# Turning the rotated keys and queries with transposing DMAs on planes of 16-bit words

## The chip, the cores and the metric

The kernel runs on one core of one Trainium2 chip. The metric is the device time of one execution in microseconds, taken as the median of repeated runs. A run's profile gives a span, from the first to the last instruction, which is a little shorter than the device time. The engines are called as in the profile: PE is TensorE's matmul side and PEld its weight loads, DVE is VectorE, ACT is ScalarE, POOL is GpSimd, and SP is SyncE, which only issues DMAs here.

## The reference

The reference is a two-layer decoder trunk on 256 tokens of width 1024, all in float32. Layer 0 is a gated short convolution, a cross-attention to 256 memory tokens and a SwiGLU. Then the residual stream gives one shared set of keys and values (8 heads of 128). Layer 1 is a block-sparse causal attention that reads them, a second cross-attention and a second SwiGLU. At 256 tokens the block-sparse attention has a single block, so it is plain causal attention inside that block. What matters here, cut to its core:

```python
k, v = jnp.split(rms_norm(x, kv_norm) @ w_kv, 2, axis=-1)
k = apply_partial_rope(k.reshape(bsz, seq, N_HEADS, HEAD_DIM), cos, sin)
q = apply_partial_rope((h @ w_q).reshape(bsz, seq, N_HEADS, HEAD_DIM), cos, sin)
...
s_own = jnp.einsum("bhqd,bhkd->bhqk", q_c, k_own).astype(jnp.float32) * scale
```

The rotation touches the first 32 of each head's 128 features. The products of queries and keys contract over the 128 features, so both operands are needed with features on the partitions, while the projections leave tokens on the partitions. The step between the two is a transposition of 128x128 float32 blocks, and that step is what the change rewrites.

## The kernel before

Every large product is done with three matmuls on split operands: each operand is a high part (rounded to the matmul's float32r) and a low part (the rest), and a product is high x low, low x high and high x high (`mm3`, line 338). Weights come in chunks of 128 rows x 1024 columns (512 KB): a load on SP's queue into one of 5 raw buffers, a high part written by ACT, a low part written by DVE (`split_high`, `split_low`), and both parts go into one of 10 weight buffers (`WBUFS`).

The program is written as one long order of PE work. Beside it a planner in Python keeps an estimated clock for each engine (`Clock`), and puts all other work in between. Side jobs are generators (`Side`): a job emits some instructions, yields, and is taken up again when the planner's clock says that they are done. After nearly every matmul the planner polls the jobs that are due, and then lets the weight feed go on (`Feed.pump`): one low part if DVE is free by the planner's clock, and one high part if ACT is. A pause can stand in the feed's way:

```python
    # Side.poll, lines 146-147
        soon = any(self.clock.now <= i[0] <= self.clock.now + HOLD for i in self.open)
        self.feed.pump(soon)
    # Feed.pump, lines 214-215
        if soon and sum(it["halves"] for it in self.items[self.taken:self.lows]) >= AMPLE:
            return
    # arrived, lines 316-318
        while clock.ready(ap) > clock.now != seen:
            seen = clock.now
            yield 200
```

`HOLD` is 300 ns and `AMPLE` is 2. A job that has yielded a number of nanoseconds is due that much later, so `soon` says that some job is due within 300 ns. `halves` is 1 for each chunk of the projections k1, q1 and v1. `taken` counts the chunks that PE has begun to use and `lows` those that are split completely. If a chunk is wanted that has not been split, `Feed.take` emits its missing parts at once. When a low part is emitted, the load of the chunk five further on follows on SP's queue (`load_to`), where it waits until DVE has read the raw buffer.

The stage around the change is `moba` (line 1480). It runs the projections k1, q1 and v1 one after the other with `proj_rows`: token half h=0 over all 8 chunks, each chunk for both column banks b=0 and 1, and then h=1 over the same chunks, of which the first five bankwise together and the last three bank by bank. So a projection takes its 8 chunks in its first half, 6 matmuls each, and takes none in its second half, in which the chunks are given back one after the other. Each of the four results (h, b) of k1 and q1 is 128 tokens x 512 features, which is four heads. `turn` evicts it with ACT into the tile `r`, with the normalisation's factor, rotates it in place on DVE (four instructions, tile `rope`), turns its four 128x128 blocks with four PE transposes into one PSUM bank (`pt_r`), and copies that bank into `kT` or `qT`: on ACT for b=0, on DVE for b=1. There are 8 such turns. `attend` (line 1517) is started for (h, pair of heads) from the beginning of v1 on, 4000 ns apart by the planner's clock; it needs the turned keys and queries of its heads and, later, the values. The "half" tiles, 8 of them, hold `r` and the softmax's tiles.

DMA is booked by the planner as well: a weight load takes 1.55 ns for each of its 1024 columns (line 350), one after the other, and the DRAM-to-DRAM copies that prepare sums of weights for a later stage (lines 464 and 466, tile `T`) take 1460 or 3300 ns.

Of the kernel before, what the change touches and what calls it, by code (L numbers as in the profile page):

```python
# [12 lines left out]
F32R = mybir.dt.float32r  # L13
BF16 = mybir.dt.bfloat16
I32 = mybir.dt.int32
AF = mybir.ActivationFunctionType
OP = mybir.AluOpType
AX = mybir.AxisListType

P = 128  # L20
# [65 lines left out]
class Timed:  # L86
# [5 lines left out]
    def __getattr__(self, op):  # L92
        call = getattr(self.engine, op)

        def issue(out, *args, **kw):
# [5 lines left out]
            for func in args:  # L101
                if func in (AF.Exp, AF.Silu, AF.Sin) and func != self.clock.table:
                    self.clock.table = func
# [160 lines left out]
def yoco_kernel(  # L264
# [6 lines left out]
    nc = tc.nc  # L271
# [16 lines left out]
    clock = Clock()  # L288
    vector, scalar, pool = (Timed(clock, n, e) for n, e in
                            (("dve", nc.vector), ("act", nc.scalar), ("pool", nc.gpsimd)))  # L290
    side = Side(clock, tp=2, gu=2, half=HALVES, pair=PAIRS)
# [8 lines left out]
    def tp_tile(name):  # L300
        return ps_tp.tile([P, 4, P], F32, tag="tp", name=name)
# [5 lines left out]
    def held_half(name, shape=(P, 512)):  # L307
        return halves.tile(list(shape), F32, tag="half", name=name)
# [4 lines left out]
    def arrived(ap):  # L313

        seen = None
# [3 lines that stand above are left out]
# [4 lines left out]
    def tok(h):  # L323
        return slice(h * P, (h + 1) * P)
# [9 lines left out]
    def transpose(o, i):  # L334
        nc.tensor.transpose(o, i, ident[:i.shape[0], :i.shape[0]])
        clock.note("pe", 109, [o], [i], 200)
# [55 lines left out]
    def split_high(it, raw):  # L392
        hi = wts.tile([P, it["a"], it["b"]], F32R, tag="hi", name=f"hi_{it['name']}")
        lo = wts.tile([P, it["a"], it["b"]], F32R, tag="lo", name=f"lo_{it['name']}")
        for c in chunk_pieces(it):
            if it["gain"] is None:
                scalar.copy(hi[:, :, c], raw[:, :, c])
            else:
                scalar.activation(hi[:, :, c], raw[:, :, c], AF.Copy, scale=gain_col(*it["gain"]))
        return hi, lo  # L400
# [150 lines left out]
    def proj_rows(act, name, done, order=STRAIGHT):  # L551

        chunks, accs = {}, {}
        for h, k, b in order:
            if (h, b) not in accs:
                accs[h, b] = acc_tile(f"acc_{name}_{h}_{b}")
            if k not in chunks:
                chunks[k] = feed.take(f"{name}_{k}")
            if h == 1 and b == 1:
                feed.free()  # L560
            mm_rows(accs[h, b], act, k, h, chunks[k], b, k == 0, k == KD - 1)
            if k == KD - 1:
                done(h, b, accs[h, b])

    def turn_parts(src, dst, h, g, gain=None):

# [25 lines left out]
    def square_half(src, ss, b):  # L592
        junk = small.tile([P, 512], BF16, tag="junk", name="junk", bufs=2)
        scalar.activation(junk[:, :src.shape[1]], src, AF.Square, accum_out=ss[:, b:b + 1])

# [12 lines left out]
    def keep(dst, acc, scale, b):  # L608
        if b == 0:
            scalar.activation(dst, acc, AF.Copy, scale=scale)  # L610
        else:
# [15 lines left out]
    def gain_col(name, k):  # L627
        i = GAINS.index(name) * KD + k
        return g_cols[:, i:i + 1]
# [26 lines left out]
    class Turned:  # L656
# [24 lines left out]
        def turn(self, i, t):  # L681
            yield from arrived(t)
            for k in range(2):
                scalar.activation(t[:, k, :], t[:, k, :], AF.Copy, scale=gain_col(self.gain, 2 * i + k))
            yield
# [140 lines left out]
    def mem_values(name, mT):  # L826
        vs = [acts.tile([P, 2, D], F32R, tag="unit", name=f"{name}_{h}") for h in range(2)]

        def keep_parts(h, b, acc):
            hi, lo = (vs[h][:, r, bank(b)] for r in range(2))  # L830
            scalar.activation(hi, acc, AF.Copy, scale=m_rs[:, h:h + 1])
            yield
# [84 lines left out]
    def angles():  # L917
        freq = const.tile([P, HR], F32, name="freq")
        for i in range(HR):
            nc.gpsimd.memset(freq[:, i:i + 1], inv_freq[i])  # L920
        pos_i = const.tile([P, 2], I32, name="pos_i")
        with nc.allow_non_contiguous_dma(reason="256 positions"):
# [557 lines left out]
    def moba(src, into):  # L1480
        act = src.act
        kT = unit_f32("kT", [P, NH, T])
        v_sb = unit_f32("v_sb", [P, 2, D])
        qT = unit_f32("qT1", [P, NH, T])
        scale = P ** -0.5
        turning, attending = {}, {}

        def turned(dst, key):

            def turn(h, b, acc, r):  # L1490
                scalar.activation(r, acc, AF.Copy, scale=rstd[h])
                yield
                v = r.rearrange("p (n d) -> p n d", d=P)
                t = small.tile([P, 2, 4, ROT], F32, tag="rope", name="rope", bufs=1)
                for i in range(2):
                    vector.tensor_mul(t[:, i], v[:, :, :ROT], cs[:, h, i:i + 1, :].to_broadcast([P, 4, ROT]))
                vector.tensor_sub(v[:, :, :HR], t[:, 0, :, :HR], t[:, 1, :, HR:])
                vector.tensor_add(v[:, :, HR:ROT], t[:, 0, :, HR:], t[:, 1, :, :HR])
                yield
                yield from side.hold("tp")  # L1500
                pt = tp_tile("pt_r")
                for i in range(4):
                    transpose(pt[:, i, :], r[:, i * P:(i + 1) * P])
                side.give("half")
                yield
                d = dst[:, 4 * b:4 * b + 4, tok(h)]
                if b:
                    vector.tensor_copy(d, pt)
                else:
                    scalar.copy(d, pt)  # L1510
                side.give("tp")

            def done(h, b, acc):
                turning[key, h, b] = side.start(turn(h, b, acc, half_tile("r")))
            return done

        def attend(h, hp, oT):
            m = (h + 1) * P
            for hh in range(h + 1):
                for key in "qk":  # L1520
                    side.finish(turning[key, hh, hp // 2])
            yield from side.hold("gu")
            s = gu_tile("s1")
            for i in range(2):
                n = 2 * hp + i
                mm(s[:, i, :m], qT[:, n, tok(h)], kT[:, n, :m], True, True, 218 * (h + 1))
            yield
            own = s[:, :, h * P:m]
            vector.tensor_add(own, own, causal[:, None, :].to_broadcast([P, 2, P]))
            yield from side.hold("half")  # L1530
            p = held_half("p1", (P, 2, T))
            yield from softmax(s[:, :, :m], p[:, :, :m], scale, -scale)
            yield from side.hold("tp")
            pt = tp_tile("pt1")
            for i in range(2):
                for kt in range(h + 1):
                    transpose(pt[:, 2 * i + kt, :], p[:, i, kt * P:(kt + 1) * P])
            side.give("half")
            yield from side.hold("half")
            pT = held_half("pT1", (P, 2, 2, P))  # L1540
            yield
            scalar.copy(pT[:, :, :h + 1, :], pt.rearrange("p (i k) t -> p i k t", i=2)[:, :, :h + 1, :])
            side.give("tp")
            yield
            c = slice(hp * 2 * P, (hp + 1) * 2 * P)
            while any((hh, hp // 2) not in v_jobs or clock.ready(v_sb[:, hh, c]) > clock.now for hh in range(h + 1)):
                yield 100
            yield from side.hold("tp")
            po = tp_tile("po1")
            for i in range(2):  # L1550
                n = 2 * hp + i
                for kt in range(h + 1):
                    mm(po[:, i, :], v_sb[:, kt, n * P:(n + 1) * P], pT[:, i, kt, :], kt == 0, kt == h, 218)
            side.give("half")
            yield
            u, j0 = oT.units[hp // 2], 2 * (hp % 2)
            yield from split_steps(u[:, j0:j0 + 2, 0, tok(h)], u[:, j0:j0 + 2, 1, tok(h)], po[:, :2, :])

        proj_rows(act, "k1", turned(kT, "k"))
        proj_rows(act, "q1", turned(qT, "q"))  # L1560
        mT1 = Act(side, [])

        def mem_bank(g):
            mT1.units.append(acts.tile([P, 4, 2, T], F32R, tag="unit", name=f"mT1_{g}"))
            nc.gpsimd.dma_start(mT1.units[g], mem_aside[g])

        mem_bank(0)
        oT = new_act("oT_moba")

        def attend_all():  # L1570
            yield 1500
            for h in range(2):
                for hp in range(4):
                    attending[h, hp] = side.start(attend(h, hp, oT))
                    yield 4000

        every = side.start(attend_all())
        v_jobs = {}

        def keep_v(h, b, acc):  # L1580
            keep(v_sb[:, h, bank(b)], acc, rstd[h], b)
            v_jobs[h, b] = True

        proj_rows(act, "v1", keep_v)
        mem_bank(1)
        memk1 = mem_keys("memk1", mT1, (1, 1, 3000, 6000))
        side.finish(every)
        for job in attending.values():
            side.finish(job)
        proj_rows(oT, "o1", residual(into))  # L1590
        return memk1, mT1
# [81 lines left out]
```

## Time and profile before

| what | value |
|---|---|
| device time, median of 3 runs | 788.64 us (787.6 to 789.31) |
| profiled execution, span | 785.8 us, 11249 instructions |
| profiled execution, own total time | not listed by the profile; the timed runs lie 1.8 to 3.5 us above the span |
| busy: PE, PEld | 775.1 us (99%), 664.4 us (85%) |
| busy: DVE, ACT, POOL | 572.7 us (73%), 458.3 us (58%), 41.5 us (5%) |
| DMA | 182.71 MB, mean 233 GB/s |
| first matmul of k1, q1, v1, memk1 | 387.5, 411.1, 435.1, 465.3 us |

Busy shares are means over the whole span. A row of a timeline reads: start in us, duration in us, engine, line of the kernel, operation, output <- inputs, shape, and how many instructions were merged; a bracket gives the idle time before it and what ended it. A row of a group reads: busy time in us and mean ns of one. The lines 107, 331, 335 and 348 are those of helpers that record every DVE, ACT or POOL instruction, every matmul, every PE transpose and every load, so a reader goes by the tiles' names. The chain of waits is followed back from the last instruction, and gives for each piece what the end of the program hung on at that time.

### The profile page before, as it was taken

What the parts mean: (1) busy time and instruction counts of PE and PEld (TensorE: products, weight loads), DVE (VectorE), ACT (ScalarE), POOL (GpSimd) and SP (SyncE); (2) the same over time, 40 slices, a digit from 0 to 9 for tenths busy, and PEclk for the clock granted to TensorE, in tenths of its full rate; (3) what the DMA queues carried; (4) which work ended last, traced back from release to release, by engine and by line L of the source; (5) the groups of instructions that cost most, each with busy time, mean ns of one, the idle gap of its engine ahead of it and who ended that gap; (6) DMA issues with size and microseconds to landing.
All of it is one profiled execution on the core that took longest, in us unless ns stands there. A gap on an engine that the chain in (4) does not pass through costs nothing.

```text
span 785.8 us, 11249 instructions
## 1 busy us (share of the span) xinstructions
PE 775.1 (99%) x4151; PEld 664.4 (85%) x4151; DVE 572.7 (73%) x863; ACT 458.3 (58%) x728; POOL 41.5 (5%) x68
## 2 busy tenths in 40 slices
PE   8999999999999999999999999999999999999996
PEld 7988888898788888888888889888987888888885
DVE  5988787768687566687766666876767786876874
ACT  6875656575564455566655563655755556655651
POOL 1000001100100000000110010021101000000000
PEclk9999999999999999999999999999999999999999
DMA  8887788926676855699789666989956856856931
GB/s 316 298 272 217 249 303 228 353 75 214 191 235 231 242 170 191 205 346 351 235 246 294 194 160 187 322 229 267 255 185 185 247 175 212 309 193 210 335 119 53
DMA packets 99959, 182.71 MB, mean 233 GB/s; under 512 B 6656, under 2 KB 62976, under 8 KB 99456
## 3 DMA queue, kind: packets, MB, share of 16 engines
q1 hardware_dynamic: 92656, 167.02, 62.4%
q0 software_dynamic: 6816, 14.68, 10.6%
q8 instruction: 32, 0.52, 0.3%
q10 hardware_dynamic: 432, 0.29, 0.1%
q14 instruction: 23, 0.19, 0.1%
HBM read 178.82 MB, written 28.31 MB: 264 GB/s over the span
## 4 chain that ended last, share of the span: by engine, by line
PE 91%; DVE 2%; DMA 1%; issue 1%; ACT 1%; POOLq 0%; DVEq 0%; ACTq 0%
PE gu L331 20%; PE ff L331 14%; PE seven L331 7%; PE q_acc L331 6%; PE acc_mo L331 6%; PE acc_memv L331 6%; PE cu L331 5%; PE acc_memk L331 3%; PE acc_v L331 3%; PE pb L331 3%; PE acc_q L331 3%; PE acc_o L331 3%; PE acc_cout L331 3%; PE acc_k L331 3%; PE po L331 2%; PE s L331 2%
## 5 line engine op out<-in xcount | busy, mean ns | idle before, releaser
L331 PE MATMUL ff<-hi_wd,guT 128*128 128x512 f32 (+1 forms) x352 | 108.3, 388 | 0.0
L331 PEld LDWEIGHTS ff<-hi_wd,guT 128*128 128x128 f32 x352 | 65.8, 188 | 12.8
L331 PE MATMUL ff<-lo_wd,guT 128*128 128x512 f32 (+1 forms) x176 | 68.3, 388 | 0.0
L107 DVE TENSOR_TENSOR gu_sb<-gu_sb,gu 128x256 f32<-128x256 f32 x48 | 20.2, 421 | 56.1 <-ACT gu_sb L107 55.4
L107 ACT COPY gu_sb<-gu 128x256 f32<-128x256 f32 x48 | 17.9, 373 | 72.2 <-PE gu L331 72.1
L107 DVE TENSOR_TENSOR lo_wd<-raw_wd,hi_wd 128x1024 fp32r<-128x1024 f32 x44 | 53.5, 1220 | 2.5 <-ACT hi_wd L107 2.4
L107 ACT CAST hi_wd<-raw_wd 128x1024 fp32r<-128x1024 f32 x44 | 46.0, 1049 | 8.0 <-DMA raw_wd<-in_ffn_w_down_dram 6.7
L331 PE MATMUL gu<-ffn,hi_wg 128*128 128x512 f32 x192 | 48.0, 390 | 0.0
L331 PE MATMUL gu<-ffn,hi_wu 128*128 128x512 f32 x192 | 47.7, 391 | 0.0
L331 PE MATMUL acc_memk<-mT,hi_memk 128*128 128x256 f32 x256 | 46.2, 286 | 0.2 <-ACT hi_memk L107 0.2
L331 PEld LDWEIGHTS gu<-ffn,hi_wg 128*128 128x128 f32 x192 | 35.9, 188 | 7.3
L331 PEld LDWEIGHTS gu<-ffn,hi_wu 128*128 128x128 f32 x192 | 35.7, 188 | 7.2
L331 PE MATMUL gu<-hi_wr,ffn 128*128 128x512 f32 x128 | 40.8, 395 | 0.0
L331 PE MATMUL acc_mo<-hi_mo,oT_mem 128*128 128x512 f32 x128 | 40.6, 393 | 0.0
L107 DVE TENSOR_TENSOR lo_wu<-raw_wu,hi_wu 128x1024 fp32r<-128x1024 f32 x32 | 38.7, 1221 | 2.6 <-ACT hi_wu L107 2.5
L331 PEld LDWEIGHTS acc_memk<-mT,hi_memk 128*128 128x128 f32 x256 | 39.5, 193 | 0.8 <-ACT hi_memk L107 0.6
L331 PE MATMUL acc_memv<-hi_memv,mT 128*128 128x512 f32 x128 | 39.6, 390 | 0.0
L464 POOL DMA_DIRECT2D T<-in_ffn_w_gu_dram x24 | 25.6, 1068 | 256.6 <-DMA T<-in_ffn_w_gu_dram 87.9
L331 PEld LDWEIGHTS ff<-lo_wd,guT 128*128 128x128 f32 x176 | 33.2, 188 | 6.3
L107 ACT CAST hi_wu<-raw_wu 128x1024 fp32r<-128x1024 f32 x32 | 33.6, 1052 | 5.4 <-DMA raw_wu<-in_ffn_w_gu_dram 4.5
L331 PE MATMUL acc_memk<-mT,lo_memk 128*128 128x256 f32 x128 | 35.1, 288 | 0.8 <-DVE lo_memk L107 0.7
L107 POOL TENSOR_TENSOR rs<-ms,neg_half 128x1 f32<-128x1 f32 x14 | 12.3, 878 | 414.7 <-DVE ms L107 414.7
(267 smaller groups left out, 1967.9 us busy)
## 6 DMA issues: line engine op xcount, KB each, us to landing
raw_wd<-in_ffn_w_down_dram SPq DMA_DIRECT2D x44, 512.0 KB, 5.1
T<-in_ffn_w_gu_dram POOLq DMA_DIRECT2D x24, 512.0 KB, 8.4
raw_wg<-in_ffn_w_gu_dram SPq DMA_DIRECT2D x24, 512.0 KB, 5.3
raw_wu<-in_ffn_w_gu_dram SPq DMA_DIRECT2D x24, 512.0 KB, 4.9
raw_wT<-T SPq DMA_DIRECT2D x24, 512.0 KB, 4.9
raw_wB<-in_ffn_w_gu_dram SPq DMA_DIRECT2D x18, 512.0 KB, 5.2
raw_memv<-in_mem_w_kv_dram SPq DMA_DIRECT2D x16, 512.0 KB, 6.2
raw_mq<-in_mem_w_q_dram SPq DMA_DIRECT2D x16, 512.0 KB, 6.3
```

The costliest lines, as they stand in the source:

```text
L107: return call(out, *args, **kw)
L331: nc.tensor.matmul(o, l, r, start=start, stop=stop)
L464: nc.gpsimd.dma_start(dst, src, accum_op=OP.add)
```

## The change

The four PE transposes and the copy out of PSUM go. In their place `turn_by_dma` does this for each of the 8 turns:

1. A DVE copy takes the rotated tile, 128 tokens x 512 float32, as 1024 16-bit words a row, and writes the words into two planes: first all first halves of the numbers, then all second halves (tile `planes`).
2. One transposing DMA, issued from SP's queue, turns the 8 blocks of 128 words of the planes, so that features come to the partitions (tile `turned`).
3. A second DVE copy interleaves the two planes again into `kT` or `qT`.

Both copies are on DVE in all 8 turns. Between the steps the job waits with `arrived`, and the planner books the DMA at 1500 ns and its result at 4000 ns behind that. `attend` no longer finishes the turns that it needs; it waits for them, and for their results, by polling every 200 ns.

```diff
+    def copy_words(engine, out, src, out_f32, src_f32):
+        fixed, each = clock.COST[engine]
+        if engine == "act":
+            nc.scalar.copy(out, src)
+        else:
+            nc.vector.tensor_copy(out, src)
+        clock.note(engine, fixed + each * math.prod(out.shape[1:]), [out_f32], [src_f32])
+
+    def turn_by_dma(src, dst, engines):
+        yield from side.hold("half")
+        flat = held_half("planes")
+        copy_words(engines[0], flat.bitcast(U16).rearrange("p (two n) -> p two n", two=2),
+                   src.bitcast(U16).rearrange("p (n two) -> p two n", two=2), flat, src)
+        side.give("half")
+        yield from side.hold("half")
+        back = held_half("turned")
+        yield from arrived(flat)
+        words = back.bitcast(U16).rearrange("p (b t) -> p b t", t=P)
+        nc.sync.dma_start_transpose(words, flat.bitcast(U16))
+        clock.note("dma", 1500, [back], [flat], 4000)
+        side.give("half")
+        yield from arrived(back)
+        copy_words(engines[1], dst.bitcast(U16).rearrange("p n (t two) -> p two n t", two=2),
+                   words.rearrange("p (two n) t -> p two n t", two=2), dst, back)
+        side.give("half")
+        yield
...
-                yield from side.hold("tp")
-                pt = tp_tile("pt_r")
-                for i in range(4):
-                    transpose(pt[:, i, :], r[:, i * P:(i + 1) * P])
-                side.give("half")
-                yield
-                d = dst[:, 4 * b:4 * b + 4, tok(h)]
-                if b:
-                    vector.tensor_copy(d, pt)
-                else:
-                    scalar.copy(d, pt)
-                side.give("tp")
+                yield from turn_by_dma(r, dst[:, 4 * b:4 * b + 4, tok(h)], ("dve", "dve"))
...
             for hh in range(h + 1):
-                for key in "qk":
-                    side.finish(turning[key, hh, hp // 2])
+                for dst, key in ((qT, "q"), (kT, "k")):
+                    while not turning[key, hh, hp // 2][2]:
+                        yield 200
+                    while clock.ready(dst[:, 2 * hp:2 * hp + 2, tok(hh)]) > clock.now:
+                        yield 200
```

More of the change, by code (lines that the diff above doesn't have):

```diff
@@ L15 @@
 I32 = mybir.dt.int32
+U16 = mybir.dt.uint16
 AF = mybir.ActivationFunctionType
```

## The prediction

> **What bounds the kernel now.** I read the page first, then the chain of waits around the change, then the timelines of ACT and DVE there.
>
> ```profile
> span 785.8 us, 11249 instructions
> PE 775.1 (99%) x4151; PEld 664.4 (85%) x4151; DVE 572.7 (73%) x863; ACT 458.3 (58%) x728; POOL 41.5 (5%) x68
> PE 91%; DVE 2%; DMA 1%; issue 1%; ACT 1%; POOLq 0%; DVEq 0%; ACTq 0%
> ```
>
> PE is busy for 99% of the span and carries 91% of the chain. So PE work that is removed shortens the run, and a PE wait that is added lengthens it; other work counts only when it makes PE wait. The chain in order of time (start, us, what) prices the removed work:
>
> ```profile
> 400.73 0.44 PE pt_r L335 x4
> ...
> 401.64 0.53 PE pt_r L335 x4
> 402.17 9.12 PE acc_k L331 x40
> ...
> 412.43 0.44 PE pt_r L335 x4
> ...
> 413.33 0.44 PE pt_r L335 x4
> 413.77 10.71 PE acc_q L331 x47
> 424.48 0.44 PE pt_r L335 x4
> ...
> 425.38 0.48 PE pt_r L335 x4
> 425.86 9.09 PE acc_q L331 x40
> 434.95 0.44 PE pt_r L335 x4
> ...
> 437.02 0.44 PE pt_r L335 x4
> ```
>
> All eight groups are on the chain: 6 x 0.44 + 0.53 + 0.48 = 3.65 us. Between them PE runs without a gap at 9.12 / 40 = 0.228 us a matmul, so a chunk of weights lasts 6 x 0.228 = 1.37 us in the first half of a projection, and the half lasts 10.9 us. That it has no gap is owed to weights split well ahead:
>
> ```profile
> 391.98 2.19 ACT L107 ACTIVATE hi_q<-raw_q,g_cols 128x1024 fp32r<-128x1024 f32 x2
> 398.79 1.31 ACT L107 ACTIVATE r<-acc_k,rs 128x512 f32<-128x512 f32 x2 [4.62 <-PE acc_k L331]
> 401.21 0.59 ACT L107 COPY kT<-pt_r 128x512 f32<-128x512 f32 x1 [1.11 <-PE pt_r L335]
> 401.69 1.16 ACT L107 ACTIVATE hi_q<-raw_q,g_cols 128x1024 fp32r<-128x1024 f32 x1
> ...
> 407.30 1.16 ACT L107 ACTIVATE hi_q<-raw_q,g_cols 128x1024 fp32r<-128x1024 f32 x1 [0.26 <-PE acc_k L331]
> ...
> 411.33 0.69 ACT L107 ACTIVATE r<-acc_k,rs 128x512 f32<-128x512 f32 x1 [1.29 <-PE acc_k L331]
> ...
> 425.44 1.16 ACT L107 ACTIVATE hi_v<-raw_v,g_cols 128x1024 fp32r<-128x1024 f32 x1
> ...
> 433.62 1.15 ACT L107 ACTIVATE hi_v<-raw_v,g_cols 128x1024 fp32r<-128x1024 f32 x1
> ```
>
> Ten weight buffers hold the 8 chunks of k1 and q_0, q_1 (the two at 391.98). The next high part comes at 401.69, right behind the copy that ends k1's first turn, and q1's chunks then follow one by one during k1's second half, q_2 at 401.69 to q_6 at 407.30. The same happens in q1's second half: v_2 to v_7 from 425.44 to 433.62. Each projection begins with seven or eight chunks split. That lead is what I look at.
>
> **The change, part by part.** *Removed:* 32 PE transposes, -3.65 us on the path. Also four ACT and four DVE copies out of PSUM:
>
> ```profile
> L107 ACT COPY kT<-pt_r x2: 587/588/588, 401.2 to 412.9; 128x512 f32<-128x512 f32 x2
> L107 DVE COPY kT<-pt_r x2: 693/693/693, 402.2 to 413.8; 128x512 f32<-128x512 f32 x2
> ```
>
> These 4 x 0.59 and 4 x 0.69 us lie beside PE and count for nothing by themselves.
>
> *Added on DVE:* 16 copies of 1024 words. No row shows a copy of 16-bit words. The nearest have one source, SBUF to SBUF:
>
> ```profile
> L107 DVE TENSOR_SCALAR p<-p,ri 128x128 f32<-128x128 f32 x8 | 1.9, 284 | 0.1
> L107 DVE TENSOR_SCALAR p<-p,ri 128x256 f32<-128x256 f32 x24 | 7.7, 363 | 0.4
> L107 DVE TENSOR_TENSOR lo_wd<-raw_wd,hi_wd 128x1024 fp32r<-128x1024 f32 x44 | 53.5, 1220 | 2.5 <-ACT hi_wd L107 2.4
> ```
>
> From 128 to 256 elements they grow by 79 ns, so 1024 elements come to 363 + 6 x 79 = 0.84 us. Upper end: one element a step as in the two-source row, 1.22 us. Lower end: four words in the time of one element, 0.36 us. I take 0.84, since these rows have the copies' operands; 16 of them are 13.4 us. [...]
>
> *Added on the DMA queue:* eight transposing DMAs of 256 KB. Nothing like them is in the trace. The nearest rows:
>
> ```profile
> raw_wr<-in_ffn_w_gu_dram SPq DMA_DIRECT2D x32, 256.0 KB, 3.6
> raw_q<-in_moba_w_q_dram SPq DMA_DIRECT2D x8, 512.0 KB, 5.4
> q1 hardware_dynamic: 92656, 167.02, 62.4%
> ```
>
> Lower end: 256 KB land in 3.6 us like a load of that size. Upper end: queue q1 took 0.624 x 785.8 x 16 / 92656 = 0.085 us of one engine a packet; if rows of 128 words, 256 B, travel one by one, a turn is 1024 packets or 5.4 us of all 16 engines. I take 5 us to landing: the planner books 1500 + 4000 ns, so a copy back stands 5.5 us or more behind its copy out in DVE's order and would not wait. On SP's queue the DMA waits for its copy out; queued behind are loads, which wait for low parts later still in DVE's order. That costs nothing.
>
> *Moved: the feed.* This decides. Before, a turn was over within 3.0 us (398.79 to 401.80). Now it waits in `arrived`, polling every 200 ns, for at least the booked 5.5 us, more where booked loads stand ahead. A job due in 200 ns is inside the 300 ns of `soon`, so as long as one turn waits, the feed stops at two split chunks. The two turns of each token half wait from about 402 to 408 or later, and the next two from about 410. So q_2 to q_6 are not split in k1's second half; q1 begins with q_0 and q_1, and the rest is split while PE uses it. v1 fares alike. The rows for the race in q1, with S = q1's start (411.1 before):
>
> ```profile
> 412.05 0.49 DVE L107 TENSOR_TENSOR rope<-r,cs 128x128 f32<-128x128 f32 x2 [1.09 <-ACT r L107]
> 412.58 0.36 DVE L107 TENSOR_TENSOR r<-rope 128x64 f32<-128x64 f32 x2
> ...
> 415.77 2.48 DVE L107 SCALAR_TENSOR_TENSOR lo_v<-raw_v,g_cols,hi_v 128x1024 fp32r<-128x1024 f32 x2
> ```
>
> k1's last result is evicted by S + 0.9 and rotated by S + 1.8; its copy out ends at S + 2.6. The high part of q_2 follows the eviction (1.16 us, S + 2.1), so q_2's low part runs from S + 2.6 to S + 3.9. Five more at 2.48 / 2 = 1.24 us are 6.2 us. Copies back of k1's turns fall among them: four if all were booked late, 3.1 us at a pitch of 0.78; two if the first pair came in time, 1.6 us. q_7 is ready at S + 11.7 to S + 13.3. PE wants it at S + 7 x 1.37 = S + 9.6. The stall is 2.1 to 3.7 us; I take 3.0. The load of q_7 agrees: it waits for q_2's low part, lands 5.4 us later at S + 9.3, and needs 1.16 + 1.28 us of splitting.
>
> In v1 the race is the same, and the attention's steps join it on DVE:
>
> ```profile
> L107 DVE TENSOR_TENSOR s<-s,causal 128x256 f32<-128x256 f32 x3 | 1.3, 429 | 2.7 <-PE s L331 2.7
> L107 DVE TENSOR_REDUCE mx<-s 128x2 f32<-128x256 f32 x3 | 1.3, 425 | 0.1
> L107 DVE TENSOR_SCALAR p<-p,ri 128x128 f32<-128x128 f32 x6 | 1.4, 284 | 0.1
> 437.45 0.45 PE s L331 x4
> ```
>
> One head pair costs DVE 0.43 + 0.43 + 2 x 0.28 = 1.4 us and gives PE 0.45 us to do meanwhile. One of them ahead of v_7, started 4 us apart: 3.0 + 1.4 - 0.45, so 4.0 us. In memk1, next, a chunk lasts longer on PE, 24 matmuls, and I add nothing.
>
> *Sum:* -3.65 + 3.0 + 4.0 = +3.4 us against the profiled execution of 785.8 us; the median of the runs is 788.64, 2.8 us around the span that the change does not touch. Forecast 792.0 us. Its own range: 2.1 us in both races gives +0.6; copies of 1.22 us (a copy out and up to four back, 5 x 0.38 = 1.9 us more a race) and two head pairs ahead of v_7 (1.0 more) give -3.65 + 5.6 + 6.6 = +8.6. So 789.2 to 797.2.
>
> **Rivals.** *The lead holds, and the change is faster.* If the planner books the DMAs soon after the copies out, the first pair of turns is over by about 408, and before the next pair waits (410) the feed has 2 us, enough for one or two chunks. Each further chunk of lead takes 1.37 us off a race, so two save 2.7 of the 3.0. From the point at which two slip in, in both projections, only the gain stays: 788.64 - 3.65 = 785.0 us. For it: DVE is idle for long here:
>
> ```profile
> 389.50:411.00 21.50, 21.50 (x101) 17.57 (x100) 15.17 (x25) 12.58 (x15) 3.68 (x3) 1.00 0.83 271
> 411.00:435.00 24.00, 24.00 (x116) 19.69 (x115) 14.92 (x26) 13.87 (x16) 1.68 (x2) 1.00 0.97 298
> ```
>
> DVE has 15.4 us free of 45.5 (third busy column), more than the 13.4 - 2.8 added. Against it: the stop is by the order written, not by a lack of DVE time, and the second pair waits across the start of q1.
>
> *Only one race is lost*, because in the other the waits end early: -3.65 + 3.0 to 4.0, so 788 to 789, no change that can be seen.
>
> *The transposing DMA is slow on its ring.* At 5.4 us each, four in a row take 22 us of a queue busy for 0.83 to 0.97 of the time (last share above). k1's four end at about 402 + 22 = 424; their copies back stand in DVE's order at about 414 to 418, ahead of q_3 to q_7. DVE waits some 6 to 10 us there, and again in v1: 792 + 12 to 20, about 808 us. [...] Against it: every load row moves 512 KB within 5.4 us of landing time. Beyond that point the turn would not do what it is said to do, free the path, at all.
>
> **How the numbers follow.** A measurement of this kernel can tell about 0.2%, 1.6 us. Forecast (both races lost): 0.52, slower. Slow ring: 0.12, slower. One race lost: 0.14, the same. Lead holds: 0.22, faster. So faster 0.22, same 0.14, slower 0.64. The range runs from 784.8, just under the clean gain, to 801, which holds the forecast's own range and the near part of the slow ring; 0.1 above and a little below are left out.
>
> **What would show it.** Right: no `pt_r`; in the first half of q1 PE waits for DVE `lo_q`, and in v1 for `lo_v`; the third `hi_q` starts only after q1's first matmul, the third `hi_v` only near v1's. Copies of words near 0.84 us, 16 of them; the transposing DMA landing within 5.5 us. Wrong: `hi_q` in k1's second half as before and no PE wait (lead holds); DVE copies to `kT` waiting for DMA by several us (slow ring); a word copy of 1.2 us or more, or a granted clock under 1.00 in the stalls, would raise the price.

## The result and the profile after

The changed kernel takes 797.18 us (796.97 to 797.75, 4 runs) against 788.87 us for the kernel before, measured beside it: a ratio of 1.0112, 95% interval 1.0100 to 1.0124, 8.3 us slower. The forecast was 792.0 us, slower by 3.4 us; its range of 784.8 to 801 holds the result, its own narrower range (789.2 to 797.2) ends there.

The page of the kernel after: span, busy times, the granted clock in 40 slices, DMA packets, the queue of SP's and ACT's transfers, and the chain.

```profile
span 795.9 us, 11191 instructions
PE 776.2 (98%) x4119; PEld 662.9 (83%) x4119; DVE 579.2 (73%) x875; ACT 455.3 (57%) x724; POOL 41.8 (5%) x68
PEclk9999999999999999999999899999999999999999
DMA packets 108407, 184.81 MB, mean 232 GB/s; under 512 B 15104, under 2 KB 71424, under 8 KB 107904
q1 hardware_dynamic: 101104, 169.12, 63.3%
PE 82%; DVE 5%; DMA 5%; issue 2%; ACT 2%; POOLq 0%; DVEq 0%; ACTq 0%; SPq 0%
```

PE's share of the chain falls from 91% to 82%, and DVE and DMA take 5% each: PE now waits. One slice of the clock row has an 8. To find where, take the first use of a low part in each stage. These are the groups by tile of the kernel before, then of the kernel after, between 384 and 512 us (minimum, median and maximum in ns, first and last start in us):

```profile
L331 PE MATMUL acc_k<-lo_k,moba x32: 387/389/478, 387.5 to 410.4; 128*128 128x512 f32 x32
L331 PE MATMUL acc_q<-lo_q,moba x32: 389/389/476, 411.1 to 434.1; 128*128 128x512 f32 x32
L331 PE MATMUL acc_v<-lo_v,moba x32: 389/393/485, 435.1 to 463.7; 128*128 128x512 f32 x32
L331 PE MATMUL acc_o<-lo_o,oT_moba x25: 387/389/396, 494.0 to 511.3; 128*128 128x512 f32 x25
```

```profile
L332 PE MATMUL acc_k<-lo_k,moba x32: 389/389/477, 389.1 to 411.0; 128*128 128x512 f32 x32
L332 PE MATMUL acc_q<-lo_q,moba x32: 389/389/499, 411.6 to 435.8; 128*128 128x512 f32 x32
L332 PE MATMUL acc_v<-lo_v,moba x32: 387/392/792, 436.5 to 478.3; 128*128 128x512 f32 x32
L332 PE MATMUL acc_o<-lo_o,oT_moba x12: 389/389/396, 504.2 to 511.7; 128*128 128x512 f32 x12
```

From the start of k1 to the start of o1 the kernel before takes 494.0 - 387.5 = 106.5 us and the kernel after 504.2 - 389.1 = 115.1 us: +8.6 us, the whole difference. By stage: k1 23.6 to 22.5, q1 24.0 to 24.9, and v1 with what follows it 58.9 to 67.7. The 3.65 us of transposes left these stages, so 8.6 + 3.65 = 12.2 us of new loss are to be explained: 3.0 us in q1 (24.9 less 96 matmuls x 0.228 us) and 9.2 us from v1 on. Below, "the stage" is this stretch from k1 to o1. Its start moves by up to 1.9 us between profiles, also for kernels that are alike up to it, so I compare its length.

What PE waited for in the timeline of the kernel after (in brackets the gap and what ended it):

```profile
414.99 0.50 PE L332 MATMUL acc_q<-lo_q,moba 128*128 128x512 f32 x1 [0.47 <-DVE lo_q L108]
418.05 0.50 PE L332 MATMUL acc_q<-lo_q,moba 128*128 128x512 f32 x1 [1.40 <-DVE lo_q L108]
...
444.61 0.50 PE L332 MATMUL acc_v<-lo_v,moba 128*128 128x512 f32 x1 [3.37 <-DVE lo_v L108]
447.06 0.79 PE L332 MATMUL acc_v<-lo_v,moba 128*128 128x512 f32 x1 [0.62 <-DVE lo_v L108]
457.67 0.50 PE L332 MATMUL acc_v<-lo_v,moba 128*128 128x512 f32 x1 [1.32 <-DVE lo_v L108]
```

Every gap ends with a low part, as the forecast said. The matmul at 447.06 takes 0.79 us where the others take 0.39 to 0.50. The windows of the kernel after show why (PE, PEld, DVE, ACT and POOL busy, then the granted clock, the DMA share, GB/s):

```profile
440.00:445.00 5.00, 1.63 (x8) 1.01 (x7) 2.95 (x4) 1.66 (x2) 0.00 (x0) 1.00 0.96 197
445.00:450.00 5.00, 4.38 (x17) 3.45 (x16) 4.39 (x8) 1.64 (x2) 0.00 (x0) 0.59 1.15 348
450.00:455.00 5.00, 5.00 (x23) 4.08 (x22) 4.50 (x13) 4.48 (x11) 0.00 (x0) 0.72 0.68 243
```

Behind the gap of 3.37 us the granted clock is 0.59 and then 0.72: (0.41 + 0.28) x 5 = 3.45 us of PE time are lost while PE counts as busy. From v1 on, the gaps (5.5 us in all in the view of waits) and the lost clock make 9.0 of the 9.2 us.

And why the low part at 444.61 was late, in DVE's and SP's timelines of the kernel after:

```profile
438.24 1.28 DVE L108 SCALAR_TENSOR_TENSOR lo_v<-raw_v,g_cols,hi_v 128x1024 fp32r<-128x1024 f32 x1
442.05 0.69 DVE L572 COPY planes<-r 128x1024 uint16<-128x1024 uint16 x1 [2.53 <-DMA turned<-planes]
442.66 0.73 DVE L572 COPY qT<-turned 128x1024 uint16<-128x1024 uint16 x1
443.28 1.27 DVE L108 SCALAR_TENSOR_TENSOR lo_v<-raw_v,g_cols,hi_v 128x1024 fp32r<-128x1024 f32 x1
```

```profile
419.84 10.59 SPq L349 DMA_DIRECT2D raw_v<-in_w_kv_dram  x6
432.49 9.74 SPq L586 DMA_TRANSPOSE turned<-planes  x3
442.34 0.52 SPq L349 DMA_DIRECT2D raw_v<-in_w_kv_dram  x1
```

SP had issued six loads of raw v and then stood for 9.74 us on three transposing DMAs, one of which took 7.03 us to issue. DVE's fourth copy out for the queries waited 2.53 us for one of those DMAs to finish, and the next low part of v stood behind that copy. The last load of raw v left SP at 442.34 only.

### The profile page after: what moved, and what is told of

Same layout as the page of the kernel before. It is cut to its first block, busy times and chain, and to the rows that moved or that the text cites. A ratio compares the mean times of both kernels' runs of the same rounds, so it can differ in the third digit from the quotient of the medians.

```text
span 795.9 us, 11191 instructions
## 1 busy us (share of the span) xinstructions
PE 776.2 (98%) x4119; PEld 662.9 (83%) x4119; DVE 579.2 (73%) x875; ACT 455.3 (57%) x724; POOL 41.8 (5%) x68
## 2 busy tenths in 40 slices
DMA packets 108407, 184.81 MB, mean 232 GB/s; under 512 B 15104, under 2 KB 71424, under 8 KB 107904
## 3 DMA queue, kind: packets, MB, share of 16 engines
q1 hardware_dynamic: 101104, 169.12, 63.3%
## 4 chain that ended last, share of the span: by engine, by line
PE 82%; DVE 5%; DMA 5%; issue 2%; ACT 2%; POOLq 0%; DVEq 0%; ACTq 0%; SPq 0%
PE gu L332 20%; PE ff L332 13%; PE q_acc L332 6%; PE acc_mo L332 6%; PE acc_memv L332 5%; PE seven L332 5%; PE cu L332 5%; PE acc_memk L332 3%; PE pb L332 3%; PE acc_o L332 3%; PE acc_cout L332 3%; PE acc_k L332 3%; PE acc_v L332 2%; PE s L332 2%; PE po L332 2%
## 5 line engine op out<-in xcount | busy, mean ns | idle before, releaser
L332 PE MATMUL ff<-hi_wd,guT 128*128 128x512 f32 (+1 forms) x352 | 108.2, 388 | 0.0
```

The lines of the kernel that those rows point to most:

```text
L332: nc.tensor.matmul(o, l, r, start=start, stop=stop)
```

## Experiments

*Theory A*: the polling waits stop the feed, and the late low parts follow from that alone. *Theory B*: the transposing DMAs themselves cost it, by SP's queue and the DMA engines. For each run the text on record is shown, then the result. Ratios are against the kernel before, measured beside the run. Its medians lie between 788.14 and 788.87 us, so a difference between two runs that were not measured together can carry some 0.7 us of that. "Stage" is the length from k1 to o1 in its profile (before: 106.5 us).

**1. The turns wait without polling.** The waits of `turn_by_dma` yield the whole remaining time in one piece, so they count as due soon only in their last 300 ns.

```diff
-        yield from arrived(flat)
+        yield from quiet(flat)      # yields clock.ready(ap) - clock.now
...
-        yield from arrived(back)
+        yield from quiet(back)
```

> The turns wait for the planned end of a step in one piece instead of every 200 ns, so they no longer stop the weight feed; the attention's polls stay. Theory A (the stopped feed makes the stalls): q1 loses its 3 us of stalls; in v1 the polls of the attention still stop the feed for a while, so a part of the v1 stalls stays; about 790 us, between 786 and 793. Theory B (the transposing DMAs on SP's queue and ring make them, the feed does not matter): no change, 796 to 798 us.

792.31 us, ratio 1.0050 (1.0033 to 1.0067), stage 109.2 us. 4.9 us of the 8.3 are gone, all gaps in q1 among them.

**2. `attend` too looks only every 1000 ns.**

```diff
-                        yield 200
+                        yield 1000
```

> As the run before, and the attention polls every 1000 ns instead of every 200. Theory A: the chunks of q1 and v1 are split ahead as in the kernel before, PE waits for lo_q and lo_v vanish, and the 3.65 us of the removed transposes stay as a gain: 785 to 787 us. Theory B: 796 to 798 us, with the long PE wait in v1 and the drop of the granted clock behind it as they are.

791.34 us, 1.0039 (1.0027 to 1.0052), stage 107.7 us: a little better, but theory A expected 785 to 787. Something else holds some 5 us. PE has one gap left that matters, and SP still stands on the transposing DMAs (PE's and SP's timelines of this kernel):

```profile
446.32 0.50 PE L332 MATMUL acc_v<-lo_v,moba 128*128 128x512 f32 x1 [2.69 <-DVE lo_v L108]
```

```profile
424.51 10.17 SPq L593 DMA_TRANSPOSE turned<-planes  x2
434.77 0.53 SPq L349 DMA_DIRECT2D raw_v<-in_w_kv_dram  x1
```

**3. The polls alone.** In the kernel before, with its PE transposes, each turn also starts a job that does nothing but poll every 200 ns for 13 us of the planner's clock.

```diff
+            def poller():
+                end = clock.now + 13000
+                while clock.now < end:
+                    yield 200
...
+                side.start(poller())
```

> The kernel before with its PE transposes, and beside each of the 8 turns a job that emits nothing and polls every 200 ns for 13 us of the planner's clock. Theory A: the lead in q1 and v1 shrinks to two chunks and the stalls come without any transposing DMA and without any word copy, 3 us in q1 and 3 to 6 in v1: 793 to 798 us. Theory B: no instruction is added, 788 to 789.5 us.

792.44 us, 1.0053 (1.0038 to 1.0068), stage 110.5 us. Nothing is computed or moved that was not before, and 4.2 us are lost: waits that only look at a clock cost this much here. As in the changed kernel, the third high part of q1 stands behind q1's start, which is at 413.3 (ACT's timeline of this kernel):

```profile
414.21 5.31 ACT L107 ACTIVATE hi_q<-raw_q,g_cols 128x1024 fp32r<-128x1024 f32 x5
```

This is the clearest sign for theory A, a little below its range. The loss is not where it was expected, though: q1 is 1.2 us longer than before (25.2 against 24.0) in place of 3 us, and v1 with what follows it 2.5 us (61.4 against 58.9).

**4. The changed kernel without its DMAs**, polls as they are; keys and queries stay rotated but not turned.

```diff
-        nc.sync.dma_start_transpose(words, flat.bitcast(U16))
...
-        words = back.bitcast(U16).rearrange("p (b t) -> p b t", t=P)
+        words = flat.bitcast(U16).rearrange("p (b t) -> p b t", t=P)
```

> The changed kernel without the eight transposing DMAs: the copy back reads the planes, so keys and queries are not turned and the attention computes with wrong operands; order, bookings and copies stay. Theory A: the feed is stopped as before, q1 keeps about 3 us of stalls and v1 about 4, and only what the DMA itself delayed in v1 goes (the wait of 2.5 us for the planes' buffer, the late last load, the lowered clock): about 792 us, 790 to 794. Theory B: all stalls go, 785 to 786 us.

792.60 us, 1.0059 (1.0044 to 1.0074), stage 111.3 us. The gaps in q1 are as in the changed kernel; in v1 there are five short ones (4.2 us, the longest 1.37) in place of the long one, and the clock stays at 1.00. So in the polled order the DMAs cost 4.6 us. The gaps in v1 are only 1.3 us longer in all with them (5.5 against 4.2); with the one long gap comes the lowered clock, 3.45 us. With 4.2 us for the polls alone, both theories had a part.

**5, 6, 7. What is left with quiet waits.** *Theory D*: the transposing DMAs on SP's queue and ring. *Theory C*: the word copies on DVE, and softmaxes bunched behind the waits. Run 5 takes the DMAs out of run 2 (same edit as in run 4); run 6 issues them from ACT's queue; run 7 turns only the keys by DMA, and the queries by PE transposes as before.

```diff
# run 6
-        nc.sync.dma_start_transpose(words, flat.bitcast(U16))
+        nc.scalar.dma_start_transpose(words, flat.bitcast(U16))
# run 7
+                if key == "k":
+                    yield from turn_by_dma(r, dst[:, 4 * b:4 * b + 4, tok(h)], ("dve", "dve"))
+                    return
+                yield from side.hold("tp")
+                pt = tp_tile("pt_r")
...
```

> The changed kernel with both quiet waits (the turn and the attend yield without polling) and without its eight transposing DMAs, so keys and queries are rotated but not turned; everything else, the word copies on VectorE included, is as in the run with both quiet waits (791.3 us). Theory D (what is left there comes from the transposing DMAs standing on SP's queue behind the loads of raw v): 784.5 to 786.5 us, below the kernel before by the 32 PE transposes taken away, and no wait of PE for lo_v over 1 us. Theory C (it comes from the word copies on VectorE and the softmax bunched behind the quiet attends): 790 to 791.5 us, with the 2.7 us wait for lo_v still there.

791.40 us, 1.0045 (1.0030 to 1.0060), stage 108.5 us: no better than with the DMAs. Theory D falls for this order. What holds the low part is the order written, as the timelines of ACT, DVE and PE of this kernel show:

```profile
433.83 3.22 ACT L108 ACTIVATE hi_v<-raw_v,g_cols 128x1024 fp32r<-128x1024 f32 x3
```

```profile
439.10 1.38 DVE L572 COPY qT<-planes 128x1024 uint16<-128x1024 uint16 x2
442.99 0.43 DVE L108 TENSOR_TENSOR s<-s,causal 128x256 f32<-128x256 f32 x1 [2.51 <-PE s L332]
...
443.99 0.43 DVE L108 TENSOR_TENSOR s<-s,causal 128x256 f32<-128x256 f32 x1
...
444.99 1.28 DVE L108 SCALAR_TENSOR_TENSOR lo_v<-raw_v,g_cols,hi_v 128x1024 fp32r<-128x1024 f32 x1
```

```profile
446.33 0.80 PE L332 MATMUL acc_v<-lo_v,moba 128*128 128x512 f32 x1 [2.70 <-DVE lo_v L108]
```

The last high part of v is ready at 437.05, and DVE stands idle from 440.5 to 443.0. But the low part is written behind the first steps of two softmaxes, which wait for PE's scores. It could have run some 4 us earlier.

> The changed kernel with both quiet waits, and the eight transposing DMAs issued from ScalarE's queue in place of SP's. Theory D, if SP's blocked issue is what costs: the last load of raw v is issued some 7 us earlier, 786 to 788 us. Theory D, if it is the load on the DMA engines that the two kinds of transfers share: 789 to 791 us, with raw v landing as late as before. Theory C: 790 to 791.5 us.

792.89 us (788.7 to 799.56), 1.0058 (1.0030 to 1.0085). Its ten runs spread over 11 us, why is open, and the profile is of one at 795.52 us. The standing moves with the instruction: ACT is held where SP was, and its next high part waits 8.19 us (ACT's timeline of this kernel).

```profile
424.71 7.98 ACTq L593 DMA_TRANSPOSE turned<-planes  x2
432.79 1.15 ACT L108 ACTIVATE hi_v<-raw_v,g_cols 128x1024 fp32r<-128x1024 f32 x1 [8.19 <-issue]
```

> The changed kernel with both quiet waits, but only the keys are turned by DMA; the queries are turned by 16 PE transposes as before, so no transposing DMA meets the loads of raw v. Theory D: 786 to 787.5 us, the gain of four transposition groups (4 x 0.44 us) and no stall in the stage of v, faster than the kernel before. Theory C: 788 to 790 us, the word copies of the keys and the quiet attends costing what they did.

786.67 us (10 runs) against 788.14, ratio 0.9980 (0.9971 to 0.9990), stage 104.4 us. It is faster than both kernels, by about the four groups taken out (4 x 0.44 = 1.8 us), and PE has no gap that waits for a low part. Four transposing DMAs and eight word copies beside the loads cost nothing here, though the slowest of the four takes 9.7 us to land and one issue holds SP for 6.61 us.

**8, 9, 10, 11. Polls gone, and the booking.** *Theory E*: the planner books each transposing DMA with 1500 ns on the loads' account, so it believes the last raw v late and writes its parts behind the softmaxes. Run 8: all waits of the changed kernel yield -1, so they are asked at every poll and never count as soon. Run 9: run 8 with the DMAs booked on an account of their own. Run 10: run 9 without the DMAs. Run 11: run 9 with the keys alone.

```diff
# runs 8 to 11
-            yield 200
+            yield -1
# runs 9 to 11
-        clock.note("dma", 1500, [back], [flat], 4000)
+        clock.note("turn", 0, [back], [flat], 4000)
```

> The changed kernel, in which no wait for a turned block counts as soon any more: both loops are asked at every poll, but the feed is never stopped for them (with 1000 ns between two looks, several open attends can still stop it). Theory A (what is left with both quiet waits is still the stopped feed): 785 to 787.5 us. Theory E (what is left comes from the booking: each transposing DMA is written into the planner's DMA account with 1500 ns, so raw v 7 is believed to land late and its high and low words are written behind two softmaxes): 789.5 to 792 us, since the booking is untouched and lo_v 7 still stands behind the two softmaxes.

790.75 us, 1.0028 (1.0014 to 1.0042), stage 107.1 us. So the polls were worth 797.18 - 790.75 = 6.4 us of the changed kernel, and the rest is not theirs: one gap of 2.70 us is left, at the same place as in run 5.

> As the run before it, and the transposing DMAs are booked on an account of their own (landing 4000 ns after the planes are written), no longer on that of the loads, so lo_v 6 and 7 are written ahead of the later softmaxes. Theory E alone: 784.5 to 787 us, faster than the kernel before. Theory D (the DMAs on SP's queue behind loads of raw v also cost by themselves): 788 to 793 us, with VectorE waiting some us for a turned block that lands after 7 to 10 us and lo_v behind it.

791.77 us, 1.0049 (1.0031 to 1.0066), stage 108.2 us. The low parts stand earlier, but now the copies back stand too early, and DVE waits for the transfers (waits of this kernel between 390 and 500 us: total, times, longest):

```profile
DVE kT L572 <- DMA turned<-planes: 6.6, 3, 4.0
DVE qT L572 <- DMA turned<-planes: 4.3, 2, 2.9
```

> The same order as the run before it without the eight transposing DMAs (keys and queries are rotated but not turned). Theory E: 784.5 to 786 us, no wait of PE for lo_v over 1 us: the order is repaired and nothing waits for a transfer. Theory C (the word copies on VectorE cost by themselves): 788 us or more. The difference from the run before it is the price of the DMAs alone.

788.55 us, 1.0004 (0.9995 to 1.0014), stage 104.6 us. On record this is theory C's time (788 or more), and E's 784.5 to 786 us without a wait over 1 us is missed. The comparisons give both a part: the order is worth 791.40 - 788.55 = 2.9 us without the DMAs (run 5 against this one, measured apart), and the DMAs cost 791.77 - 788.55 = 3.2 us in this order. One gap of 1.66 us is left. The stage is 1.9 us shorter than before, the time is not. Behind the stage there are 786.5 - 493.4 = 293.1 us, against 291.8 before. But that part takes 291.6 to 293.3 us over all the profiles here, so one profile doesn't settle why.

> Only the keys turned by DMA, with waits that never stop the feed and the own booking; queries by 16 PE transposes as before. All theories: 785.5 to 787 us, near the 786.7 us of the keys alone with the quiet waits; under 786 if the booking cost something there too.

791.40 us, 1.0039 (1.0024 to 1.0053), stage 107.4 us: more than 4 us above the range on record. The keys' copies back, believed to land after 4 us, hold DVE in q1, and PE's transposes of the queries wait (view of waits of this kernel):

```profile
DVE kT L572 <- DMA turned<-planes: 6.5, 3, 4.1
...
PE pt_r L336 <- DVE r L108: 1.7, 2, 1.3
```

**12. Keys alone, with the polls of the changed kernel** (run 7 with `yield 200` and `arrived`).

> The changed kernel with its own waits (200 ns between two looks), but only the keys turned by DMA; the queries by 16 PE transposes as before. The twin of the run with quiet waits and the keys alone (786.7 us): only the polls differ. Theory A (the polls stop the feed and that alone costs): 789.5 to 793 us, the stall of about 3 us in the stage of q as in the changed kernel, and the rest of the loss in the stage of v only as far as attends still poll there. If the loss belongs to the queries' DMAs among the loads of raw v instead: 786 to 788 us, with no stall over 1 us in the stage of q.

796.61 us, 1.0108 (1.0091 to 1.0125), stage 112.8 us: 3.6 us above theory A's range, and far from the 786 to 788 us of the other reading. The gaps of 0.47 and 1.40 us in q1 are back, as in the changed kernel; later a group of transposes waits 2.19 us for a rotated query (PE's timeline), and the clock falls to 0.66 behind it (windows):

```profile
429.55 0.63 PE L336 MATMUL pt_r<-ident,r 128*128 128x128 f32 x4 [2.19 <-DVE r L108]
```

```profile
430.00:435.00 5.00, 5.00 (x19) 3.96 (x18) 3.56 (x7) 2.88 (x4) 1.17 (x2) 0.66 1.06 341
```

Between this kernel and run 7 only the waits differ: 796.61 against 786.67, 9.9 us, measured apart but beside kernels before that agree (788.24 and 788.14). That is theory A's direction in a pair by itself; the size was set too low. 6.8 us of it lie in q1 (29.9 us against 23.1), where 3 had been expected.

## Why the prediction was right, and where it was not

*The gain, -3.65 us.* Right. Where nothing else is lost it shows: run 7, with half of it, has a stage 2.1 us shorter for a forecast 1.8. In run 10, with all of it, the stage is 1.9 us shorter with a gap of 1.66 us in it, 3.6 us together.

*The feed stops.* Right, and it is the main cause: 6.4 us by run 8, 9.9 us in the pair of runs 7 and 12. ACT's timeline of the kernel after has what was asked for:

```profile
393.53 2.18 ACT L108 ACTIVATE hi_q<-raw_q,g_cols 128x1024 fp32r<-128x1024 f32 x2
...
412.47 4.26 ACT L108 ACTIVATE hi_q<-raw_q,g_cols 128x1024 fp32r<-128x1024 f32 x4
```

q_0 and q_1 are split at 393.53, and the third chunk comes at 412.47, behind q1's start at 411.6. The same sign for v1 did not come: its third high part starts at 430.59, 5.9 us ahead of v1's first matmul at 436.5. Only its third low part, at 438.24, is behind it.

*The race in q1, +3.0 us.* Right: 3.0 us by the stage. q_7 is split at 424.0, 12.4 us behind q1's start, inside the forecast's 11.7 to 13.3, with a copy out and four copies back on the way. The gaps come earlier than at q_7, at the third and fourth chunk (0.47 and 1.40 us). The view of waits puts 2.0 of the 3.0 us down as gaps; where the rest lies it doesn't say.

*The race in v1, +4.0 us.* The mechanism was there, the size was not: 9.2 us. The term that failed is "queued behind are loads, which wait for low parts later still in DVE's order. That costs nothing", with the 5 us to landing. The first two for the keys, with no load just ahead of them, landed in 3.0 to 3.5 us; the first two for the queries, behind six loads of raw v, in 9.1 to 9.5 us, and one issue held SP for 7.03 us. Whether the loads ahead on the queue made them late, or engines shared with other queues (their share is 1.15 from 430 to 440 us), no run separates. Then the next copy out waited 2.53 us for its buffer, and the low part behind it made the gap of 3.37 us. Without the DMAs (run 4) that long gap is absent and 4.6 us come back. The forecast had put a softmax ahead of the last chunk. That came too, at 457.67, with a gap of 1.32 us; but what came late first was the fourth chunk, behind a word copy.

*The granted clock.* It was named as what would raise the price, and set at nothing in the sum. It cost 3.45 us of the 9.2.

*The size.* That the result lies at the upper end of the forecast's own range (+8.6 us) is luck in part. That end was made of copies of 1.22 us and of one more head pair ahead of v_7; the copies were shorter than forecast, and the excess came from the wait for the transposing DMA and from the clock, which that end didn't hold. The 2.8 us that the forecast put around the span are not all around it either: each execution of the kernel after lies 1.7 to 1.9 us above its own span, and 785.8 + 1.8 = 787.6 us is the fastest run of the kernel before. The difference of +3.4 us doesn't rest on this.

*Word copies, 0.84 us.* A little high (groups by tile of the kernel after):

```profile
L572 DVE COPY planes<-r x8: 682/686/695, 402.9 to 442.1; 128x1024 uint16<-128x1024 uint16 x8
L572 DVE COPY kT<-turned x4: 736/741/752, 415.5 to 422.1; 128x1024 uint16<-128x1024 uint16 x4
L586 SPq DMA_TRANSPOSE turned<-planes x8: 1232/1264/7027, 403.6 to 443.0; - x8
```

0.69 us out and 0.74 us back.

*The rivals.* "The lead holds" did not happen with polls: they see to it. With the waits quiet the lead does hold, and then it needs the queries left on PE (run 7) for a gain. "Slow ring" had a true core, the landing behind the loads, at 4.6 us (run 4) in place of 12 to 20. What was put against it, that every load row moves 512 KB within 5.4 us, doesn't hold for the kernel before: there the 8 loads of `raw_v` have a median of 7.4 us to landing. "One race lost" did not happen.

*Still open.* With quiet waits and all eight turns, the loss goes back to a gap of 2.7 us, its clock, and the written order (runs 5 and 8; in run 10, with the order changed, the gap is 1.66 us). Each booking tried moved the wait: too long, and low parts stand behind softmaxes; too short, and DVE stands on a transfer. A booking that follows the 2.7 to 9.5 us that the landings took in the kernel after wasn't tried. Nor was it shown why run 10 is not faster in time as its stage is.

## What to carry to other kernels

Where a planner writes the order, a wait is part of the program: ask which of its rules a waiting job sets off, since polling alone cost 4.2 us in a kernel that did nothing else new. Work taken off the bounding engine paid here only where nothing urgent stood behind the work that replaced it: the same transposing DMAs cost nothing for the keys alone (run 7, 786.67 us against 788.14), nor for all eight with quiet waits (run 2 against run 5, 791.34 against 791.40 us), and 4.6 and 3.2 us where DVE's next low part stood behind a copy that waited for one of them (the kernel after against run 4, run 9 against run 10). And price a stall with the clock behind it, not by its gap alone: after the gap of 3.37 us the lowered clock cost 3.45 us more.

## What the runs showed of the hardware

**The clock behind a short gap.** In windows of 1 us the granted clock of the kernel after is 0.50 from 446 to 452 us and 1.00 again from 453. The time lost to it came in two sizes: 3.45 us after a gap of 3.37 us (after) and 3.4 us after one of 3.3 us (run 6: (0.43 + 0.25) x 5), and 1.7 us after gaps of 2.70 (run 5), 2.19 (run 12) and 1.87 us (run 9: 0.75 and 0.91 in two windows, (0.25 + 0.09) x 5). After 1.66 us (run 10) nothing was lost, but nothing either after a second gap in run 6, of 2.7 us: PE is idle for 2.36 us of the window from 450 to 455, and the clock is 1.00 in it and in the next. So the length of a gap alone doesn't decide it. The windows of run 5 and of run 10:

```profile
445.00:450.00 5.00, 3.67 (x15) 3.35 (x16) 3.89 (x12) 3.70 (x12) 0.00 (x0) 0.66 0.64 207
```

```profile
445.00:450.00 5.00, 5.00 (x31) 4.31 (x31) 4.74 (x15) 2.58 (x9) 0.00 (x0) 1.00 0.87 293
```

**The transposing DMA.** Queue q1 has 101104 - 92656 = 8448 packets more, all under 512 B (15104 - 6656): 1056 for each, near the 1024 of the forecast's upper end. Its time on the engines grew from 0.624 x 785.8 x 16 = 7846 us to 0.633 x 795.9 x 16 = 8061 us, so 215 / 16 / 8 = 1.7 us of all 16 engines for 256 KB, a third of that upper end, since a packet took 215 / 8448 = 0.025 us and not 0.085. 256 KB in 1.7 us are 154 GB/s, an estimate from times in which packets of other queues moved too; no run here moves a turn alone.

**An issue that holds its engine.** The instruction took 1.23 to 1.37 us on seven issues and 7.03 us on one (SP, after); ACT was held 7.98 us by two of them in run 6. On both queues the engine that issues it stood still meanwhile. The long issue is the second of two: the first, behind six loads, was issued in 1.27 us and landed after 9.5 us, and the second, 1.4 us behind its start, held SP for 7.03 us. In six other runs with these DMAs on SP the longest issue and the longest landing were 8.68 and 12.2 us (run 1), 8.58 and 11.8 us (run 2), 6.61 and 9.7 us (run 7), 9.21 and 11.7 us (run 8), 3.86 and 7.0 us (run 9) and 1.37 and 6.2 us (run 11).
